# An encoder layer on one core: tiles at multiples of 512 bytes, late v and bias tables, and the second FFN matrix mixed in four products

## The chip, the cores and the metric

The kernel runs on one core of a Trainium2 chip. The metric is the device time of one execution in microseconds (us). Work is done by five engines with queues of their own: TensorE (PE, matmuls; the loading of its stationary operand is shown apart as PEld), VectorE (DVE), ScalarE (ACT), GpSimd (POOL) and SyncE (SP), whose queue here issues nearly all DMA transfers. Engines wait for each other by semaphores.

## The reference

One layer of an encoder, 1024 tokens of width 1024, float32:

```python
mod = c_act @ w_ada[l] + b_ada[l]                      # shifts, scales and gates: sh1 sc1 gt1 sh2 sc2 gt2
h = rms_norm(x, g_norm1[l]) * (1.0 + sc1) + sh1
proj = h @ w_in[l]                                     # q, k, v of both attentions, and the gates
o_a = neighbourhood_attention(qa, ka, va, rpb[l])      # 8 heads, with a table of biases
outs, lses = dilated_window_attention(...)             # 3 groups of 4 heads
o_b = einsum('gbsh,gbshd->bshd', softmax(lses), outs)  # "combine"
gate_a, gate_b = split(sigmoid(gates + b_gate[l]))
merged = gate_a * (o_a @ w_proj_a[l]) + gate_b * (o_b @ w_proj_b[l])
x = x + gt1 * (merged @ w_o[l])
h2 = rms_norm(x, g_norm2[l]) * (1.0 + sc2) + sh2
a, up = split(h2 @ w_ffn_in[l])                        # d_ff = 2816
x = x + gt2 * ((silu(a) * up) @ w_ffn_out[l])
```

## The kernel before

Matrices are multiplied as sums of three products of split halves: `wsplit` makes of a float32 tile a rounded tile `whi` (on ACT, L108) and the rest `wlo` (on POOL or DVE, L109), and `PASS` runs hi x hi, hi x lo and lo x hi into one bank of PSUM. A matmul has a stationary operand of 128 columns and a moving operand of up to 512.

The stages, in order of time:

- Attention, to about 616 us. Ten units u (two heads each; kinds 0 to 2 are the dilated groups, kind 3 the neighbourhood attention) of eight token tiles t; n = 8u + t counts the steps. Each step projects one tile of q, k and v (L293) and, between its matmuls, runs the scores (L451, L518), transposes (L477, L543) and value products (L492, L563) of an earlier unit. DVE also works off the adaLN matrix (`ada_step`: loads `wa` by L276, accumulates by L282). The results of kinds 0 to 2 are combined by `combine_prep` and `combine_step` (transposes L647) from step n = 63 on.
- Gates (L687, L706), projections of the attention outputs (L1095, moving tile oT), output projection (L1237, moving tiles wr and whi, wlo), to 876 us.
- First FFN product (L1301, moving tiles h2T and t), to 1302 us. Both FFN products use a fast scheme with seven block products in place of eight; t are mixed blocks of h2T.
- Second FFN product (L1471), to the end: seven products, numbered n = 0 to 6 in `PRODS`, each of 11 steps k, each step 12 matmuls. Products 0 to 2 use blocks of the second matrix as they are; products 3 to 6 use mixes of them, made by `w2_mix(k)`: four loads `m` on SP (L1445) and four subtractions on DVE (L1447 to L1450), called inside products 1 and 2. `finish` multiplies a finished block by the gate (DVE, L1492), adds x (POOL, L1493) and stores it.

PE's order is the order of the code. For ACT, DVE, POOL and SP a scheduler sets the order, except where instructions are pinned by `pin`, which keeps them in program order.

Memory: a pool on the left begins where the pool left of it ends, a pool on the right ends where the pool right of it begins. Counted from a multiple of 512 bytes, the tiles of the left pools (raw, whi, wlo, hT, h2T) begin at byte 320. Those of the right pools begin at 480 in the stages behind attention (tg, oT, wr, sg, the mixed t, e, m), and in attention at 352 (qk, PT, and all tiles of tag "big") or 416 (P, stg), with qn at 0. All right-hand tiles of 512-column matmuls lie above byte 139,000 of a partition, all left-hand ones under 122,000.

The tag "big" has eight slots of 4 KB, which v, the bias tables `rb`, `wa2`, `tp`, `gsig` and others take in turn. A new unit takes its slot for v, and for kind 3 two slots for the bias tables, when it begins (t = 0); v is written to memory tile by tile and read back into that slot at t = 7 (L340, L344).

## Time and profile before

| | |
|---|---|
| median of 3 runs | 1522.92 us (1522.58 to 1523.85) |
| profiled execution | 1524.07 us, its span 1522.3 us |
| PE busy | 1499.0 us, 98% of the span |
| DVE / ACT / POOL busy | 1101.9 / 657.4 / 538.4 us |
| granted TensorE clock, mean | 0.998 |
| memory traffic | 241.66 MB, 159 GB/s over the span |

The span runs from the first to the last instruction; the execution's time has about 2 us more around it. A duration of a matmul in the trace is longer than the time until the next one starts, because matmuls are pipelined: the time that a stage takes follows from start to start, or from a window's length over the count of matmuls in it.

### The profile page before, as it was taken

The page shows a single profiled execution, that of the slowest core. Times are in us where ns is not written, and L with a number is a line of the kernel's source. Part 1 is how long each engine was busy: PE and PEld are TensorE (multiplying, and loading weights), DVE is VectorE, ACT ScalarE, POOL GpSimd, SP SyncE. Part 2 cuts the span into 40 slices and gives each one's busy share as a digit, 9 for nine tenths or more (in the row PEclk, how much of TensorE's full clock was granted, in tenths as well). Part 3 has the DMA queues.
Part 4 walks back from the last instruction along what each step waited for, and adds up shares of the span by engine and source line. Part 5 has one row for each costly group of instructions (what it writes and reads, how often), then busy time and mean ns, then how long its engine had stood idle before and what let it go on. Part 6 is the DMA issues. An engine that isn't in the chain of part 4 may idle for free. (4 is left out here: it accounts for less than half of the span.)

```text
span 1522.3 us, 24290 instructions
## 1 busy us (share of the span) xinstructions
PE 1499.0 (98%) x8156; PEld 1267.7 (83%) x8156; DVE 1101.9 (72%) x2318; ACT 657.4 (43%) x1638; POOL 538.4 (35%) x540
## 2 busy tenths in 40 slices
PE   9999999999999999999999999999999999999998
PEld 7999989998888877788888888888888888887886
DVE  6868777767899845466665596788777777599468
ACT  5555555554544543236432354333222233344442
POOL 0432333311101040002342301677777775104464
PEclk9999999999999999999999999999999999999999
DMA  9625544535245165824562225345533334798342
GB/s 369 231 76 184 158 148 150 175 124 166 73 138 149 61 202 155 304 83 126 165 217 101 93 89 177 127 132 170 174 107 104 105 107 141 268 365 285 99 153 97
DMA packets 154414, 241.66 MB, mean 159 GB/s; under 512 B 26656, under 2 KB 73376, under 8 KB 153520
## 3 DMA queue, kind: packets, MB, share of 16 engines
q1 hardware_dynamic: 153136, 235.90, 47.5%
q10 hardware_dynamic: 1152, 4.19, 0.7%
q8 instruction: 65, 1.06, 0.3%
q14 instruction: 61, 0.50, 0.1%
HBM read 179.89 MB, written 60.15 MB: 158 GB/s over the span
## 5 line engine op out<-in xcount | busy, mean ns | idle before, releaser
L109 POOL TENSOR_TENSOR wlo<-raw,whi 128x512 fp32r<-128x512 f32 (+2 forms) x133 | 173.0, 1314 | 469.4 <-ACT whi L108 417.6
L108 ACT ACTIVATE whi<-raw 128x512 fp32r<-128x512 f32 (+1 forms) x348 | 204.3, 600 | 282.7 <-PE ps_s L1471 33.6
L293 PE MATMUL ps_d<-whi,hT 128*128 128x384 f32 x1152 | 311.7, 342 | 0.3 <-ACT vs L331 0.3
L109 DVE TENSOR_TENSOR wlo<-raw,whi 128x512 fp32r<-128x512 f32 (+1 forms) x215 | 181.8, 857 | 77.2 <-ACT whi L108 72.0
L293 PEld LDWEIGHTS ps_d<-whi,hT 128*128 128x128 f32 x1152 | 210.4, 189 | 5.8 <-ACT vs L331 4.1
L293 PE MATMUL ps_d<-wlo,hT 128*128 128x384 f32 x576 | 193.9, 337 | 2.2 <-DVE wlo L109 1.9
L293 PEld LDWEIGHTS ps_d<-wlo,hT 128*128 128x128 f32 x576 | 109.0, 189 | 3.0 <-DVE wlo L109 2.2
L108 ACT ACTIVATE whi<-ws 128x512 fp32r<-128x512 f32 x65 | 40.9, 629 | 130.3 <-DVE ws L1318 76.6
L1251 POOL TENSOR_TENSOR e<-e,c 128x512 f32<-128x512 f32 x44 | 68.6, 1560 | 64.3 <-DVE c L1381 40.1
L109 POOL TENSOR_TENSOR wlo<-m,whi 128x512 fp32r<-128x512 f32 x35 | 51.6, 1484 | 54.0 <-ACT whi L108 54.0
L323 POOL TENSOR_TENSOR ra<-qn,rtab 128x64 f32<-128x64 f32 x48 | 16.2, 338 | 150.8 <-DVE qn L316 132.1
L530 ACT ACTIVATE P<-P,st 128x256 f32<-128x256 f32 (+2 forms) x100 | 45.5, 456 | 40.6 <-DVE st L528 40.6
L687 PE MATMUL ps_d<-hT,whi 128*128 128x512 f32 x192 | 60.5, 396 | 0.0
L1301 PE MATMUL ps_v<-h2T,whi 128*128 128x512 f32 x192 | 59.3, 390 | 0.0
L1301 PE MATMUL ps_s<-h2T,whi 128*128 128x512 f32 x192 | 59.2, 390 | 0.0
L466 ACT ACTIVATE P<-P,sx 128x384 f32<-128x384 f32 (+1 forms) x64 | 37.0, 578 | 51.4 <-DVE sx L465 51.4
L1249 ACT ACTIVATE e<-e 128x512 f32<-128x512 f32 x44 | 27.4, 630 | 71.9 <-DVE e L1384 47.4
L282 DVE SCALAR_TENSOR_TENSOR acc<-wa,cact,acc 128x512 f32<-128x512 f32 x56 | 42.0, 749 | 20.6 <-DMA wa<-in_wada_dram 20.4
L1301 PE MATMUL ps_d<-h2T,whi 128*128 128x512 f32 x184 | 56.8, 390 | 0.0
L109 DVE TENSOR_TENSOR wlo<-ws,whi 128x512 fp32r<-128x512 f32 x45 | 50.5, 1123 | 8.2 <-ACT whi L108 8.2
L119 ACT ACTIVATE ry<-ss,eps 128x4 f32<-128x4 f32 (+1 forms) x88 | 26.3, 299 | 67.4 <-DVE ss L314 65.2
L1250 DVE TENSOR_TENSOR e<-e 128x512 f32<-128x512 f32 x44 | 42.6, 975 | 17.3 <-ACT e L1249 17.1
(445 smaller groups left out, 3968.9 us busy)
## 6 DMA issues: line engine op xcount, KB each, us to landing
raw<-in_w_dram SPq DMA_DIRECT2D x139, 256.0 KB
ga_d<-e SPq DMA_DIRECT2D x77, 256.0 KB
raw<-ga_d SPq DMA_DIRECT2D x77, 256.0 KB
wa<-in_wada_dram SPq DMA_DIRECT2D x32, 512.0 KB
raw<-in_wqkv_dram SPq DMA_DIRECT2D x80, 192.0 KB
m<-in_w_dram SPq DMA_DIRECT2D x44, 256.0 KB
raw<-in_wg_dram SPq DMA_DIRECT2D x42, 256.0 KB
xt<-in_x_dram SPq DMA_DIRECT2D x16, 512.0 KB
```

Of the source, the lines that this page charges most:

```text
L108: nc.scalar.activation(hi[:, :n], r, AF.Copy)
L109: (eng or nc.gpsimd).tensor_sub(lo[:, :n], r, fview(hi[:, :n]))
L119: nc.scalar.activation(y, ss, AF.Ln, scale=1.0 / n, bias=eps)
L282: nc.vector.scalar_tensor_tensor(ada_acc[c], wa, cact[:, kk:kk + 1], ada_acc[c], op0=ALU.mult, op1=ALU.add)
L293: nc.tensor.matmul(pd[:, :384], tok(a, k, t), U.w[k][b][:, :384], start=(k == 0 and i == 0), stop=(k == KT - 1 and i == 2))
L466: nc.scalar.activation(P[:nq, :nk], P[:nq, :nk], AF.Exp, scale=-1.0, bias=nm, accum_out=sm)
L530: nc.scalar.activation(C.P[h][:nq, c], C.P[h][:nq, c], AF.Exp, scale=-1.0, bias=nm, accum_out=sm)
L687: nc.tensor.matmul(st["p"], gw[i, br][j][a][:, kk * 128:(kk + 1) * 128], hT[b][:, k, hs], start=(k == 0 and q == 0), stop=(k == 7 and q == 2))
L1249: nc.scalar.activation(sg, a, AF.Sigmoid)
L1250: nc.vector.tensor_mul(sg, sg, a)
L1251: nc.gpsimd.tensor_mul(sg, sg, up)
L1301: nc.tensor.matmul(pb, w[p][:, k * 128:(k + 1) * 128], b[q][:, k], start=(k == 0 and i == 0), stop=(k == 3 and i == 2))
```

## The change

It has three parts.

1. Alignment. A pool `edge` of 480 bytes is put at the right end, `rg` moves to the front of the constants, and fillers of 192, 384 and 32 bytes (`fill`) stand in the pools const, attn and wo; in attn the tags of P, PT, qn and others are taken in a fixed order at the start (`place`). With that all tiles of 512 bytes and more begin at a multiple of 512 bytes.
2. Late tables. For kinds 1 to 3 the slot of v is taken at t = 7, when v is read back, and the bias tables are taken and loaded at t = 5 (`RBT`) by `bias_tabs`. The combine begins at n = 64 (`COMB`) instead of 63.
3. Second FFN matrix. The eleven mixes are called at the steps of `MIXAT`, which lie in products 0 to 3 instead of 1 and 2. The first finished block, `finish(0, 0, c11)`, moves from behind the second product to behind the adds of the fourth, with its multiplications pinned.

```diff
+EDGE, CFILL, AFILL, OFILL = 480, 192, 384, 32
-PAIRED = 58
+PAIRED, RBT, COMB = 58, 5, 64
...
+    edge = pool("edge", "right")
+    edge.tile([128, EDGE // 4], F32, name="edge")
...
+    def fill(p, n, name):
+        p.tile([128, n // 4], F32, name=name)
...
+    rg = const.tile([128, 2, 2, 16], F32, name="rg")
+    fill(const, CFILL, "cfill")
...
+    for tag, n, bufs in (("bm", 512, 1), ("p", 512, 4), ("qn", 256, 7), ("rtab", 512, 1), ("acc2", 512, 1), ("pT", 512, 4),
+                         ("stg", 512, 3), ("vs", 128, 2), ("ra", 64, 2), ("rb", 64, 2)):
+        ap_.tile([128, n], F32, tag=tag, bufs=bufs, name="place")
...
+            if t == 7:
+                U.v = big("v", [128, 8, 128])
...
-        U.v = big("v", [128, 8, 128])
+        if U.kind == 0:
+            U.v = big("v", [128, 8, 128])
...
             U.bias = []
-            for h in range(2):
-                b = big("rb", [128, 768])
-                nc.sync.dma_start(b, rbias[U.pair * 2 + h])
-                U.bias.append(b)
         return U
+
+    def bias_tabs(U):
+        for h in range(2):
+            b = big("rb", [128, 768])
+            nc.sync.dma_start(b, rbias[U.pair * 2 + h])
+            U.bias.append(b)
...
-        ci = n - (8 * 7 + 7)
+        ci = n - COMB
...
             proj_post(U, t)
+            if U.kind == 3 and t == RBT:
+                bias_tabs(U)
+
+    fill(ap_, AFILL, "afill")
...
+    fill(wop, OFILL, "ofill")
...
+    MIXAT = tuple((n, k) for n, ks in enumerate(((4, 6, 8, 10), (2, 5, 8), (1, 4, 7), (1,))) for k in ks)
...
-            if n in (1, 2) and k % 2 == n - 1:
-                w2_mix((k + (n - 1) * HT) // 2)
+            if (n, k) in MIXAT:
+                w2_mix(MIXAT.index((n, k)))
...
-    def finish(rh, c, z, last=None):
+    def finish(rh, c, z, last=None, late=False):
...
-            nc.vector.tensor_mul(z[m], z[m], gt2[:, cs])
+            mul = nc.vector.tensor_mul(z[m], z[m], gt2[:, cs])
+            if late:
+                pin(mul)
...
     p2 = prod2(1)
     for m in range(4):
         add(c11[m], c21[m], p2[m])
-    finish(0, 0, c11)
...
     for m in range(4):
         add(c21[m], c21[m], p6[m])
         add(c12[m], c12[m], p6[m])
+    finish(0, 0, c11, late=True)
```

The order of SP at the first bias tables (end of the dilated units, about 314 us in the trace of before): v read back, the bias loads `rb`, the adaLN loads `wa`, and the stores of v's tiles `v_d`. Before:

```order
L340 DMA v<-v_d 128x1024
L398 DMA rb<-in_rbias_dram 128x768 x2
L276 DMA wa_4789<-in_wada_dram 128x1024
L276 DMA wa_4947<-in_wada_dram 128x1024
L333 DMA v_d<-vs 128x128
L276 DMA wa_5117<-in_wada_dram 128x1024
```

After (lines of the changed file: L354 is L340, L288 is L276, L416 is L398, L345 is L333):

```order
L354 DMA v<-v_d 128x1024
L288 DMA wa_4799<-in_wada_dram 128x1024
L288 DMA wa_4957<-in_wada_dram 128x1024
L288 DMA wa_5127<-in_wada_dram 128x1024
L416 DMA rb<-in_rbias_dram 128x768
L345 DMA v_d<-vs 128x128
L416 DMA rb<-in_rbias_dram 128x768
```

Three `wa` loads now stand ahead of the bias loads; the next unit (about 365 us) has the same exchange.

The order of SP at the mixes in the second FFN product: `raw<-ga_d` and `raw<-in_w` are the two operands of one step, `m` the loads of a mix. Before, from the operands of a step of product 1:

```order
L101 DMA raw<-ga_d 128x512
L101 DMA raw<-in_w_dram 128x512
L1445 DMA m_0_14800<-in_w_dram 128x512
L1445 DMA m_0_14801<-in_w_dram 128x512
L1445 DMA m_0_14802<-in_w_dram 128x512
L1445 DMA m_0_14803<-in_w_dram 128x512
L101 DMA raw<-ga_d 128x512
L101 DMA raw<-in_w_dram 128x512
```

After, at the operands of the same kind (L1467 is L1445); ahead of these rows stand the eight loads of m_0 and m_1:

```order
L1467 DMA m_2_14761<-in_w_dram 128x512
L1467 DMA m_2_14762<-in_w_dram 128x512
L1467 DMA m_2_14763<-in_w_dram 128x512
L1467 DMA m_2_14764<-in_w_dram 128x512
L1467 DMA m_3_14821<-in_w_dram 128x512
L1467 DMA m_3_14822<-in_w_dram 128x512
L1467 DMA m_3_14823<-in_w_dram 128x512
L1467 DMA m_3_14824<-in_w_dram 128x512
L111 DMA raw<-ga_d 128x512
L111 DMA raw<-in_w_dram 128x512
```

The loads of four mixes, sixteen, now stand in a row between the operands of two steps, where four stood.

POOL at the finish of c11: the adds `c<-c,x` and the splits `wlo<-m`. Before:

```order
L1260 TENSOR_TENSOR e<-e 128x512
L1493 TENSOR_TENSOR c_14496<-c_14496,x_15128 128x512
L1493 TENSOR_TENSOR c_14497<-c_14497,x_15133 128x512
L1493 TENSOR_TENSOR c_14498<-c_14498,x_15138 128x512
L1493 TENSOR_TENSOR c_14499<-c_14499,x_15143 128x512
L109 TENSOR_TENSOR wlo<-m_0_14802,whi 128x512
```

After (L1518 is L1493, L119 is L109):

```order
L119 TENSOR_TENSOR wlo<-m_5_14997,whi 128x512
L1518 TENSOR_TENSOR c_14513<-c_14513,x_15731 128x512
L1518 TENSOR_TENSOR c_14514<-c_14514,x_15736 128x512
L1518 TENSOR_TENSOR c_14515<-c_14515,x_15741 128x512
L1518 TENSOR_TENSOR c_14516<-c_14516,x_15746 128x512
L119 TENSOR_TENSOR wlo<-m_6_15081,whi 128x512
```

The four adds come 16 splits later, in the middle of those for the fifth product.

## The prediction

> **What bounds the kernel now.** I read the busy shares on the page first, then the windows by stage, then the waits of TensorE (PE), and last the durations of its matmuls by tile. The page and the windows (core, stretch, length and busy time of each engine, with the number of instructions):

> ```profile
> span 1522.3 us, 24290 instructions
> PE 1499.0 (98%) x8156; PEld 1267.7 (83%) x8156; DVE 1101.9 (72%) x2318; ACT 657.4 (43%) x1638; POOL 538.4 (35%) x540
> ...
> 314.00:530.00 216.00, 207.51 (x1463) 183.66 (x1462) 175.83 (x599) 109.99 (x381) 16.42 (x15) 0.99 0.39 119
> 616.00:1302.00 686.00, 685.10 (x3003) 558.96 (x3003) 484.51 (x640) 242.92 (x423) 320.48 (x222) 1.00 0.43 140
> 1302.00:1522.00 220.00, 212.00 (x929) 173.51 (x927) 162.11 (x213) 88.05 (x150) 83.61 (x56) 0.99 0.63 215
> ```

> PE is busy for 98% of the span and, in the gates, projections and first FFN product (616 to 1302), for 685.10 of 686 us (the row from 616). There is nothing to win there by a shorter wait; only shorter matmuls help. Outside, PE idles 8.49 us of attention's second half and 8.00 us of the last FFN stage. The waits of PE that the change could reach (us in total, times, longest):

> ```profile
> PE ps_t L477 <- DVE P L469: 2.6, 2, 1.8
> PE ps_d L1471 <- DVE wlo L109: 2.6, 3, 2.1
> PE ps_t L647 <- DVE PT L481: 1.8, 3, 1.3
> PE ps_t L647 <- ACT PT L483: 1.7, 1, 1.7
> PE ps_t L477 <- DVE rv L120: 1.3, 2, 0.8
> ```

> **Part 1, the alignment.** It adds no instruction; it moves start addresses. What that can change is in the durations of matmuls by tile (line, tiles, count: minimum/median/maximum ns). All of these move 512 columns; the moving tile is h2T, t, oT, wr, tg, or the whi and wlo of L1471.

> ```profile
> L1301 PE MATMUL ps_v<-h2T,whi x192: 389/389/476, 875.9 to 1302.5; 128*128 128x512 f32 x192
> L1471 PE MATMUL ps_d<-whi x88: 388/389/397, 1302.9 to 1511.7; 128*128 128x512 f32 x88
> L1301 PE MATMUL ps_v<-t,whi x136: 392/394/401, 945.8 to 1291.4; 128*128 128x512 f32 x136
> L1301 PE MATMUL ps_s<-t,wlo x64: 392/397/400, 951.8 to 1275.1; 128*128 128x512 f32 x64
> L1095 PE MATMUL ps_t<-oT,whi x64: 392/397/400, 714.3 to 775.7; 128*128 128x512 f32 x64
> L1095 PE MATMUL ps_s<-oT,wlo x16: 392/397/400, 721.8 to 781.5; 128*128 128x512 f32 x16
> L1237 PE MATMUL ps_d<-wr,h2T x90: 392/397/477, 781.8 to 863.7; 128*128 128x512 f32 x90
> L1237 PE MATMUL ps_v<-wr,h2T x60: 392/397/477, 808.1 to 851.7; 128*128 128x512 f32 x60
> L706 PE MATMUL ps_d<-tg,whi x40: 392/394/400, 642.3 to 700.1; 128*128 128x512 f32 x40
> L706 PE MATMUL ps_v<-tg,wlo x12: 392/398/400, 662.1 to 697.5; 128*128 128x512 f32 x12
> ```

> The median is 389 ns where the moving tile is in a left pool; where it is in a right pool, not even the minimum is under 392. Left pools begin at byte 320 of a 512-byte block, right ones of these stages at 480: the first is a multiple of 64, the second is 32 past one. Matmuls overlap, so their price is start to start. Two windows filled by one kind each give it, oT first and then whi and wlo of L1471:

> ```profile
> 719.00:775.00 56.00, 56.00 (x241) 45.02 (x240) 40.30 (x57) 25.82 (x42) 25.40 (x20) 1.00 0.49 159
> 1400.00:1500.00 100.00, 100.00 (x443) 82.84 (x442) 64.30 (x77) 42.26 (x74) 58.43 (x41) 1.00 0.42 130
> ```

> A window counts what touches it, and a 389 ns matmul at this spacing adds about 1.7: 56.00/239.3 is 234.0 ns, 100.00/441.3 is 226.6. The difference, 7.4 ns, fits the durations (medians of 394 to 398 against 389). By groups (first and last are quoted) the slow kind counts 792 with t (8 groups), 288 with oT (8), 240 with wr (3) and 180 with tg (8): 1500 matmuls. At 7.0 ns, a little under the difference since some of the fast ones too stray upward, that is 10.5 us. All of it lies in the windows in which PE never waits, so all of it is on the path; DVE and POOL keep room there (third and fifth pair of the row).

> What speaks against it: the same tiles are those at high addresses, so that the region and not the 32 bytes may be the cause, and then moving them by 32 bytes gives nothing. And the score matmuls move keys from byte 352, also 32 past a multiple of 64 and high, at the median of the projection's matmuls of the same 384 columns, which move whi from a left pool:

> ```profile
> L451 PE MATMUL ps_s<-qk x192: 274/335/445, 365.0 to 598.9; 64*128 64x384 f32 x144, 64*128 64x256 f32 x48
> L293 PE MATMUL ps_d<-whi,hT x1152: 334/334/522, 67.9 to 524.9; 128*128 128x384 f32 x192
> ```

> These run two at a time on half the rows each, so their pace may have another limit; and being high as well, they speak as much against the region as against the 32 bytes. The bounds are 0 and 11.1 us (1500 at 7.4); I take 10.5, since the step from 389 to 392 has no exception. The left pools move from 320 to 0, both multiples of 64: I book nothing for them. [...]

> **Part 2, late v and bias tables.** The 8 slots of tag "big" are shared by v, bias, adaLN weights (wa) and others. Before, a unit takes v's slot at its first tile and its bias loads (2 of 384 KB) stand on SP ahead of the wa loads. The vector engine (DVE) then stands at L282, and P's normalization L469, for which PE waits, is queued behind it:

> ```profile
> 371.93 0.75 DVE L282 SCALAR_TENSOR_TENSOR acc<-wa,cact,acc 128x512 f32<-128x512 f32 x1 [4.39 <-DMA wa<-in_wada_dram]
> 372.60 0.35 DVE L469 TENSOR_SCALAR P<-P,sx 128x256 f32<-128x256 f32 x1
> ```

> ```profile
> DVE acc L282 <- DMA wa<-in_wada_dram: 20.4, 12, 5.8
> ```

> After, wa goes first on SP. Two bias tables are 0.77 MB; at the 367 GB/s of a saturated stretch (quoted below) they took 2.1 us. Moving them behind shortens the 4.39 us wait by about that, and the 2.6 us of L477 behind L469 falls to about 0.6: 2.0 us gained. The longest wait of L282, 5.8 us, stands one unit earlier behind the same two loads, but PE loses little there; I add 0.3 us for it. Against that stands the combine, which moves one slot later: its transposes L647 wait 1.8 + 1.7 us now and may wait more or less, plus or minus 1.7. The bias tables, now issued at the sixth tile, are used by scores of the next unit, several tiles later: cover of over 10 us, nothing booked. The v loads stay at the eighth tile; their slot was taken long before and may now be held when they come: nothing booked, up to a rival. I take -2.3; the bounds are -5.6 (the waits of L477 and L647 quoted, 7.4 us, without half of L647's) and +3.5 (L647's waits double and nothing is gained).

> **Part 3, FFN2.** 44 m loads of 256 KB, 44 mix subtractions and 4 muls and 4 adds of the finish are moved, none added. Before, mixes (products 2 and 3) and the finish of block c11 meet; the timeline of DVE (start, length, instruction), of POOL and of PE (in brackets what it idled before):

> ```profile
> 1369.69 1.78 DVE L1447 TENSOR_TENSOR m<-m,m 128x512 f32<-128x512 f32 x1
> 1371.40 1.28 DVE L1492 TENSOR_TENSOR c<-c,gt 128x512 f32<-128x512 f32 x2
> 1372.60 3.45 DVE L109 TENSOR_TENSOR wlo<-raw,whi 128x512 fp32r<-128x512 f32 x2
> ```

> ```profile
> 1369.24 1.68 POOL L1493 TENSOR_TENSOR c<-c,x 128x512 f32<-128x512 f32 x1 [1.83 <-DVE c L1492]
> 1372.15 3.34 POOL L1493 TENSOR_TENSOR c<-c,x 128x512 f32<-128x512 f32 x2 [1.23 <-DMA m<-in_w_dram]
> ```

> ```profile
> 1376.10 0.50 PE L1471 MATMUL ps_d<-wlo,whi 128*128 128x512 f32 x1 [2.06 <-DVE wlo L109]
> 1382.12 0.50 PE L1471 MATMUL ps_d<-wlo,whi 128*128 128x512 f32 x1 [0.28 <-DVE wlo L109]
> ```

> The window that ends there:

> ```profile
> 1340.00:1372.00 32.00, 32.00 (x143) 26.51 (x142) 30.62 (x47) 15.10 (x24) 2.97 (x2) 1.00 1.04 379
> ```

> DVE is full (30.62 of 32 us), and beside POOL's adds its 0.68 us operations take up to 1.8 (L1447, and two of L109 take 3.45): 4 x 0.68 of muls and about 3.2 us of stretching go away from there. PE then loses neither 2.06 nor 0.28 us: 2.3. The finish lands behind product 4, in the window from 1400 quoted above, where DVE is busy for 64 and POOL for 58 of 100 us; its adds, 1.3 to 1.7 us each, fit behind wlo of L109 made several steps ahead.

> What is late next is the loads. SP's new order has 16 m loads in a row ahead of the raws of product 2's third step, where 4 stood. They begin at 1320.2:

> ```profile
> L1445 SPq DMA_DIRECT2D m<-in_w_dram x44: 327/416/1797, 1320.2 to 1385.1; - x44
> DMA packets 9257, 16.90 MB, mean 367 GB/s; under 512 B 1029, under 2 KB 1029, under 8 KB 9253
> ```

> A load takes 0.262 MB/367 = 0.71 us when DMA is full (the second row is that of 1326 to 1372). 18 of them and about 2 us of latency end at 1335.0; splitting takes 0.62 on ACT and 0.68 on DVE, and about 0.4 of queue: 1336.7. PE gets there after 13 steps of 2.72 us (12 x 226.6 ns); the first starts at 1302.9 (the row of L1471), so that makes 1338.3. The next step has four m loads ahead of its raws too: 1336.7 + 6 x 0.71 = 1341.0, against 1341.0. So the cover is about gone: a stall of 0 to 3 us, and I take 0.8, as the loads that other queues put between are not counted. Part 3: -2.3 + 0.8 = -1.5, bounds -2.3 and +0.7.

> **The sum.** -10.5 - 2.3 - 1.5 = -14.3 us. The profiled execution took 1524.07, 1.15 over the median of the runs; from the median, 1522.92 - 14.3 = 1508.6, so 1508.6 us. This case's own range is 1504 (all low ends, -19.0) to 1513 (part 1 as taken, the other two together at +0.6, half of the way to their upper ends). What tells a measurement of this kernel from no change is about 0.2%, 3.0 us.

> **Rivals.**
> Region, not alignment: the 1500 matmuls keep 234.0 ns. For it speaks that no tile in this trace is aligned and high, and the qk row; against it, that the whole step sits in the minimum of tiles in four different stages. Time: 1522.92 - 3.8 = 1519.1 (1515 to 1523). [...]

> Alignment beyond 64 bytes: matmuls from left tiles, now at byte 320, get faster as well at byte 0. If they gained as much as the right ones, 7 ns, the 924 of L1471 (77 steps of 12) alone would add 6.5 us: 1502 or below. Against it: in the rows above nothing from a left tile falls under 388 ns, and their medians are their minima, so that none of them looks delayed.

> Slower, by the v slots: eight v transfers stand on SP at the eighth tile of each unit of kinds 1 to 3 and now wait for a slot that others hold; the raws of the next unit stand behind them, and PE at the next unit's first tile. This turns the sign when it costs the 8 units 14.3 + 3.0 us, 2.2 us each, more than any single wait of PE quoted above; at 2.5 us each the time is 1522.9 - 14.3 + 20 = 1528.6. Against it: earlier wa loads free their slots sooner, and the number of slots is the same.

> **Chances.** Forecast 0.75, region 0.17, beyond 64 bytes 0.04, slower 0.03, anything else 0.01. The region's case ends more than 3.0 us faster about six times in ten, so faster is 0.75 + 0.04 + 0.10 = 0.89, same 0.07 + 0.01, slower 0.03. The range takes the forecast's own 1504 and the middle of the region's case, 1519.5: outside are 0.04, 0.03, some 0.07 of the region's and 0.04 of the forecast's tails.

> **What will show it.** Part 1: minimum 389 for t, oT, wr and tg, and about 239 to 247 matmuls in 56 us of oT. If 392 stays, the region was it. Part 2: L477's wait on L469 under 1 us, L282's waits on wa well under 20.4 us in all; a new wait of PE on v or hT's raws would be the rival. Part 3: no wait of L1471 in product 3 (1372 to 1386), and one near product 2's third to fifth step (1336 to 1346 less what part 1 and 2 gain ahead of it) of at most 3 us. The prediction is wrong if the sum of PE's idle time grows, or if the right tiles keep their duration.

## The result, and the profile after

The changed kernel takes 1513.48 us (median of 5 runs, 1512.08 to 1517.73) against 1522.92 us before (5 runs, 1522.58 to 1524.86): a ratio of 0.9938, 95% interval 0.9922 to 0.9954, 9.4 us less. The forecast was 14.3 us less. The profiled execution took 1513.48 us; its span is 10.6 us shorter than that of before, and the share and sum of PE's busy time say that all of it is busy time:

```profile
span 1511.7 us, 24292 instructions
...
PE 1488.2 (98%) x8156; PEld 1268.4 (84%) x8156; DVE 1102.9 (73%) x2318; ACT 657.5 (43%) x1638; POOL 538.7 (36%) x540
```

PE is busy for 10.8 us less, and it idles for 23.5 us, as before (23.3). By stages, from the first matmul of each (gates from 525.1 us before and 527.7 after, L706 from 616.5 and 619.1, second FFN product from 1302.9 and 1293.5, last matmul's start at 1516.2 and 1506.8):

| stage | before | after | difference | forecast |
|---|---|---|---|---|
| attention | 525.1 | 527.7 | +2.6 | -2.3 |
| gates L687 | 91.4 | 91.4 | 0 | 0 |
| L706 to L1301 | 686.4 | 674.3 | -12.1 | -10.5 |
| second FFN product, and end of the span | 219.4 | 218.2 | -1.2 | -1.5 |

Part 1, durations by tile (line numbers are those of the changed file: L1323 is L1301, L1116 is L1095), and the window that is filled with oT:

```profile
L1323 PE MATMUL ps_v<-h2T,whi x192: 389/389/476, 872.8 to 1293.0; 128*128 128x512 f32 x192
L1323 PE MATMUL ps_v<-t,whi x136: 389/389/389, 942.6 to 1282.1; 128*128 128x512 f32 x136
L1116 PE MATMUL ps_t<-oT,whi x64: 389/389/389, 715.1 to 774.5; 128*128 128x512 f32 x64
```

```profile
619.00:1293.00 674.00, 673.54 (x3004) 558.08 (x3003) 485.00 (x640) 241.45 (x423) 321.36 (x222) 1.00 0.43 142
720.00:775.00 55.00, 55.00 (x245) 45.53 (x244) 41.22 (x57) 25.01 (x41) 23.08 (x19) 1.00 0.48 158
```

The 392 to 400 ns are gone: minimum, median and maximum are 389, and 55.00/243.3 is 226.1 ns from start to start where 234.0 stood. Parts 2 and 3 show in PE's waits (L494 is L477, L1494 is L1471, L119 is L109; L672 and L675 are the combine's accumulation on DVE):

```profile
PE ps_t L494 <- DVE oacc L672: 2.8, 1, 2.8
PE ps_v L1494 <- DVE wlo L119: 2.2, 2, 1.3
PE ps_t L494 <- DVE P L486: 2.1, 2, 1.2
...
PE ps_t L494 <- DVE oacc L675: 1.9, 1, 1.9
```

The waits of the combine's transposes (1.8 and 1.7 us before) are nearly gone, and new ones stand in their place. Behind three of these waits, PE's clock is halved, in the clock record to 0.5 for 3.41 us each (stretch, length, PE busy, granted clock, DMA share, GB/s):

```profile
372.00:376.00 4.00, 2.66 (x10) 0.74 0.53 207
376.00:380.00 4.00, 4.00 (x21) 0.84 0.06 16
428.00:432.00 4.00, 3.73 (x15) 0.57 0.48 163
488.00:492.00 4.00, 3.49 (x16) 0.74 0.35 116
492.00:496.00 4.00, 4.00 (x26) 0.83 0.78 239
```

Where it is 0.5, the 384-column matmuls of L305 start every 320 ns, against 173 at full clock. What each of the three costs is estimated by (1 - clock) x length: 1.7 us. Before, there was one such place in this stage, at 372 to 380. In both profiles PE idles for 10.6 us between 100 us and the gates, so the new waits only take the place of old ones. By that estimate the 2.6 us that attention lost are 3.4 us more at half clock, less 0.8 us elsewhere. Slow matmuls count as busy time, so the idle time alone doesn't show this loss.

### The profile page after: what moved, and what is told of

Same layout as the page of the kernel before. It is cut to its first block, busy times and chain, and to the rows that moved or that the text cites. A ratio compares the mean times of both kernels' runs of the same rounds, so it can differ in the third digit from the quotient of the medians.

```text
span 1511.7 us, 24292 instructions
## 1 busy us (share of the span) xinstructions
PE 1488.2 (98%) x8156; PEld 1268.4 (84%) x8156; DVE 1102.9 (73%) x2318; ACT 657.5 (43%) x1638; POOL 538.7 (36%) x540
## 4 chain that ended last, share of the span: by engine, by line
PE 85%; DMA 6%; DVE 5%; issue 1%; ACT 1%; SPq 1%; POOL 1%; DVEq 0%; POOLq 0%; ACTq 0%
PE ps_d L305 16%; PE ps_v L1323 7%; PE ps_d L1323 7%; PE ps_s L1323 7%; PE ps_t L1323 6%; PE ps_d L704 4%; PE ps_v L1494 3%; PE ps_t L1494 3%; PE ps_s L1494 3%; PE ps_d L1494 3%; PE ps_s L1258 2%; PE ps_d L1258 2%; DMA wa<-in_wada_dram 2%; PE ps_v L1258 1%; PE ps_v L1116 1%
## 5 line engine op out<-in xcount | busy, mean ns | idle before, releaser
L119 POOL TENSOR_TENSOR wlo<-raw,whi 128x512 fp32r<-128x512 f32 (+2 forms) x133 | 172.9, 1314 | 466.6 <-ACT whi L118 437.1
L305 PE MATMUL ps_d<-whi,hT 128*128 128x384 f32 x1152 | 312.7, 343 | 0.0
L119 DVE TENSOR_TENSOR wlo<-raw,whi 128x512 fp32r<-128x512 f32 (+1 forms) x215 | 180.7, 856 | 68.8 <-ACT whi L118 67.3
L305 PEld LDWEIGHTS ps_d<-whi,hT 128*128 128x128 f32 x1152 | 211.6, 190 | 5.2 <-ACT vs L343 3.5
L305 PE MATMUL ps_d<-wlo,hT 128*128 128x384 f32 x576 | 194.5, 338 | 2.4 <-DVE wlo L119 2.0
L305 PEld LDWEIGHTS ps_d<-wlo,hT 128*128 128x128 f32 x576 | 109.5, 190 | 3.2 <-DVE wlo L119 2.3
L119 POOL TENSOR_TENSOR wlo<-m,whi 128x512 fp32r<-128x512 f32 x35 | 51.4, 1479 | 105.2 <-ACT whi L118 103.8
L335 POOL TENSOR_TENSOR ra<-qn,rtab 128x64 f32<-128x64 f32 x48 | 16.7, 349 | 153.0 <-DVE qn L328 138.0
L1271 ACT ACTIVATE e<-e 128x512 f32<-128x512 f32 x44 | 27.5, 630 | 91.4 <-DVE e L1406 64.0
L294 DVE SCALAR_TENSOR_TENSOR acc<-wa,cact,acc 128x512 f32<-128x512 f32 x56 | 43.4, 775 | 26.8 <-DMA wa<-in_wada_dram 26.8
L483 ACT ACTIVATE P<-P,sx 128x384 f32<-128x384 f32 (+1 forms) x64 | 37.1, 580 | 51.9 <-DVE sx L482 51.9
L1323 PE MATMUL ps_v<-h2T,whi 128*128 128x512 f32 x192 | 59.2, 389 | 0.0
L1323 PE MATMUL ps_s<-h2T,whi 128*128 128x512 f32 x192 | 59.1, 389 | 0.0
L1323 PE MATMUL ps_d<-h2T,whi 128*128 128x512 f32 x184 | 56.7, 390 | 0.0
L119 DVE TENSOR_TENSOR wlo<-ws,whi 128x512 fp32r<-128x512 f32 x45 | 50.2, 1116 | 8.0 <-ACT whi L118 8.0
L1272 DVE TENSOR_TENSOR e<-e 128x512 f32<-128x512 f32 x44 | 42.5, 974 | 16.7 <-ACT e L1271 16.5
```

The lines of the kernel that those rows point to most:

```text
L119: (eng or nc.gpsimd).tensor_sub(lo[:, :n], r, fview(hi[:, :n]))
L294: nc.vector.scalar_tensor_tensor(ada_acc[c], wa, cact[:, kk:kk + 1], ada_acc[c], op0=ALU.mult, op1=ALU.add)
L305: nc.tensor.matmul(pd[:, :384], tok(a, k, t), U.w[k][b][:, :384], start=(k == 0 and i == 0), stop=(k == KT - 1 and i == 2))
L483: nc.scalar.activation(P[:nq, :nk], P[:nq, :nk], AF.Exp, scale=-1.0, bias=nm, accum_out=sm)
L1272: nc.vector.tensor_mul(sg, sg, a)
L1323: nc.tensor.matmul(pb, w[p][:, k * 128:(k + 1) * 128], b[q][:, k], start=(k == 0 and i == 0), stop=(k == 3 and i == 2))
```

## The experiments

Twelve kernels ran in three rounds, each round on one chip beside the kernel before; ratios are to that kernel, so kernels of different rounds are compared by their ratios or by their traces. The first six concern the addresses.

**Alignment alone.** All edits of part 1 and none of the others; the instructions stand in the order of before on every engine.

> The kernel before with part 1 alone: all tiles at multiples of 512 bytes, the order of every queue that of before. If the start address is what makes t, oT, wr and tg slow, their matmuls have 389 ns again and the stages from 616 to 1302 us lose about 12 us in all (the changed kernel lost 1.8 + 2.2 + 1.8 + 6.3 there): 1522.9 - 12 = about 1511 us, with the waits of the attention and of the second FFN product as before. Rival: part of that came from the other two parts, and the time is 1513 us or more.

1509.72 us (1507.06 to 1510.54), ratio 0.9903 (0.9887 to 0.9919): faster than the whole change. L706 to L1301 take 673.7 us, 12.7 less than before, with t and oT at 389 ns throughout. Part 1 accounts for the whole gain and more.

**Parts 2 and 3 on the old addresses.**

> Parts 2 and 3 alone on the old addresses, the order of every queue that of the changed kernel. If the changed kernel lost the missing 5 us in the attention by itself (its start of the gates was 2.6 us later than before, with two more stretches at a granted clock of about 0.5), this one is as slow there: 1522.9 + 2.6 - 1.2 at the end = about 1524 us, between 1522 and 1526. Rival: the faster matmuls caused the new waits, and parts 2 and 3 on the old addresses gain what was forecast for them, 3.8 us: 1519 us.

1525.91 us (12 runs, 1521.53 to 1529.70), ratio 1.0014 (1.0002 to 1.0026): a little slower, as the first reading said. Attention ends at 528.4 us in its profile, with waits on `oacc` at the same two places as in the changed kernel (1.4 us at 428, 2.9 at 490). The faster matmuls did not cause them.

**An edge of 32 bytes.** Is 64 bytes the grain, as the prediction had it?

```diff
+    edge = pool("edge", "right")
+    edge.tile([128, 8], F32, name="edge")
```

> The kernel before with one edge of 32 bytes at the right end and nothing else: right tiles go from byte 480 to 448 of a 512-byte block, a multiple of 64 and not of 128 or more; left tiles stay at 320; the order is that of before. If 64 bytes are the grain, t, oT, wr and tg have 389 ns and the time is that of full alignment, about 1511 us. If 128 or 512 bytes are needed, they keep 392 to 400 ns and the time stays at about 1522 us.

1521.46 us, ratio 0.9987 (0.9974 to 1.0001). The moving tiles begin at byte 448, a multiple of 64, and are about as slow as at 480 (L1303 is L1301, L1097 is L1095):

```profile
L1303 PE MATMUL ps_v<-t,whi x136: 387/394/398, 945.8 to 1290.7; 128*128 128x512 f32 x136
L1097 PE MATMUL ps_t<-oT,whi x64: 387/394/398, 714.9 to 776.1; 128*128 128x512 f32 x64
```

So a start at a multiple of 64 bytes isn't enough: the cause that the prediction named is wrong.

**Left tiles moved away.** The changed kernel, with whi, wlo, hT and h2T at byte 480 and the right tiles left at 0.

```diff
-EDGE, CFILL, AFILL, OFILL = 480, 192, 384, 32
+EDGE, CFILL, AFILL, OFILL = 480, 160, 384, 32
```

> The changed kernel with the filler of the constants at 160 instead of 192 bytes: left tiles (whi, wlo, hT, h2T) at byte 480 instead of 0, right ones stay at 0; the order is that of the changed kernel. If a start 32 past a multiple of 64 costs 7.4 ns wherever the tile lies, the 512-column matmuls that move whi, wlo, hT or h2T (about 2650) get medians of 394 to 398 ns: +19.6 us, and if the 1776 of 384 columns in the projection pay as much, +13 us more: 1533 to 1546 us. If high addresses are needed for the loss, they keep 389 ns and the time stays at about 1513 us.

1524.95 us (one run), and neither expectation: the moved tiles stay fast and those that were not moved become slow.

```profile
L1323 PE MATMUL ps_v<-h2T,whi x192: 387/389/476, 877.6 to 1304.9; 128*128 128x512 f32 x192
L1323 PE MATMUL ps_v<-t,whi x136: 393/395/399, 947.6 to 1293.8; 128*128 128x512 f32 x136
L1116 PE MATMUL ps_t<-oT,whi x64: 393/395/399, 716.2 to 777.4; 128*128 128x512 f32 x64
```

h2T with whi, both at 480, is fast; t at 0 with whi at 480 is slow. What all runs up to here have in common is the distance from the start of the stationary tile to that of the moving one: 0 is fast (both at 0, 320 or 480, medians of 389 ns), while 32, 128 and 160 are slow (medians of 394 to 398). In these runs neither the byte itself nor the region of the memory tells the fast tiles from the slow ones.

**Edges of 160 and 416 bytes** test that distance. With 160, t, oT, wr and tg stand at 320 like whi; with 416, they stand at 64, 256 away.

> The kernel before with one edge of 160 bytes at the right end and nothing else; the order is that of before. Right tiles behind attention (tg, oT, wr, t) then begin at byte 320 of a 512-byte block, as the left ones do; neither is a multiple of 128. Theory of the run with moved left tiles: a matmul is slow when its moving tile and the stationary tile that is loaded beside it begin at different bytes of a 512-byte block. Then all of them have 389 ns and the time is that of full alignment, 1509.7 us, within 2 us. Rival: both must begin at a multiple of a larger power of two; then t, oT, wr and tg keep about 233 ns from start to start and the time is about 1521 us.

> The same with an edge of 416 bytes: right tiles at byte 64, 256 away from the left ones at 320. If what counts is the distance within 256 bytes, t, oT, wr and tg start every 226 to 227 ns and the time is 1507 to 1512 us; if it is the distance within 512 bytes, they keep 230 to 238 ns and it is 1517 to 1524 us.

```profile
L1303 PE MATMUL ps_v<-t,whi x136: 389/389/389, 941.2 to 1280.8; 128*128 128x512 f32 x136
L1097 PE MATMUL ps_t<-oT,whi x64: 389/389/389, 712.4 to 771.8; 128*128 128x512 f32 x64
```

```profile
L1303 PE MATMUL ps_v<-t,whi x136: 389/389/389, 938.4 to 1278.0; 128*128 128x512 f32 x136
L1097 PE MATMUL ps_t<-oT,whi x64: 389/389/389, 710.9 to 770.3; 128*128 128x512 f32 x64
```

The first fence is 160, the second 416; both are fast throughout. 160 took 1513.40 us (6 runs, ratio 0.9940, 0.9925 to 0.9955), 416 took 1509.54 (one run). So one tile of 416 bytes, with everything else as before, gives in its one run what the whole alignment gives, and in these runs a distance of 256 bytes is as good as 0 (389 ns), while 128 is not (394). That 160 is 3.7 us behind alignment alone (the intervals of the ratios don't overlap) is not explained by these matmuls: in its profile L706 to L1301 take 676.1 us, 1.9 of them waits. One of 0.9 us before L706 is in the kernel before too, one of 0.9 us before L1237 in no other profile. The rest of the difference stays open.

**The combine at n = 63 again**, everything else as changed.

```diff
-PAIRED, RBT, COMB = 58, 5, 64
+PAIRED, RBT, COMB = 58, 5, 63
```

> The changed kernel with the combine at n = 63 again; alignment, late tables and the new FFN order stay. If the later combine puts its DVE work (oacc) ahead of the normalization that the transposes of L494 wait for, the waits of 2.8 and 1.9 us on oacc are gone, and the stretches of halved clock behind them: about 4.7 + 3.4 us less, some 3 us of the old waits of the combine's transposes come back: 1509 to 1511 us. Rival: the late tables cause these waits; then 1513 us as the changed kernel.

1511.55 us, ratio 0.9927 (0.9915 to 0.9939) against the changed kernel's 0.9938. The waits on oacc are gone and attention ends at 525.3 us instead of 527.7; the intervals of the two ratios overlap, so the 2 us rest on the traces. There, the four profiles with the combine at n = 64 have attention end between 527.5 and 528.4 us, the two with late tables and n = 63 at 525.3 and 525.7. The mechanism is in DVE's timeline of the changed kernel (L294 is L282):

```profile
424.84 1.54 DVE L294 SCALAR_TENSOR_TENSOR acc<-wa,cact,acc 128x512 f32<-128x512 f32 x2 [4.51 <-DMA wa<-in_wada_dram]
426.29 0.68 DVE L672 TENSOR_TENSOR oacc<-ut,ps_t 128x512 f32<-128x512 f32 x1
```

DVE stands at L294 until its `wa` has landed; behind it is queued the `oacc` that empties the bank which the transposes L494 need, and PE waits 2.85 us for it. At n = 63 that pair does not meet.

**Late tables alone** (aligned, combine at 63, FFN order of before).

> Alignment and the late v and bias tables, with the combine at n = 63 and the FFN order of before. If the late tables give nothing because the adaLN step L294 is only queued earlier on DVE and waits for wa as long as before (4.5 to 5.6 us against 4.3), the time is that of alignment alone, 1509.7 us, within 1.5 us, and PE's waits between 365 and 376 us add up to 2.5 us or more. If they gain the 2.3 us that were forecast, it is 1507.4 us.

1510.43 us, ratio 0.9927 (0.9915 to 0.9940), not faster than alignment alone, and its attention ends at 525.7 us against 523.1. Counted from the start of v's loads ahead of it, `wa` is issued 1.0 us earlier than before and has landed 2.4 us earlier, about as forecast, but DVE takes the step earlier as well. The place that the prediction quoted, in the changed kernel:

```profile
368.28 0.75 DVE L294 SCALAR_TENSOR_TENSOR acc<-wa,cact,acc 128x512 f32<-128x512 f32 x1 [4.52 <-DMA wa<-in_wada_dram]
```

4.52 us of waiting where 4.39 stood. L282 now stands ahead of the scores' minimum (L482) instead of behind it, so that with late tables alone PE's wait is spread over two links (0.6 us at L468, 1.8 at L494) and not removed. The 2.6 us that this attention is longer than that of alignment alone don't show a cost of the late tables: PE idles for 8.8 us between 100 us and the gates against 9.2, and the difference is 5.1 us against 1.7 lost at half clock. The edge of 32 bytes, with the tables of before, lost 5.1 us as well.

**Part 3 undone, and part 3 alone.**

> The changed kernel with the mixes at their old steps and the finish of c11 behind the second product again. If the sixteen loads in a row cost the 2.2 to 2.5 us of waits that the changed kernel has in its second product (its 1329 to 1335 us), these go, and the old wait in the third product comes back with 0.4 us (as in the kernel with alignment alone) to 2.3 us (as before): 1511 to 1513.5 us. If part 3 gains what was forecast, 1.5 us, the time is 1515 us.

1512.63 us, ratio 0.9940 (0.9926 to 0.9953): the same as the changed kernel. The 1.3 us wait in the third product came back for the two in the second.

> Alignment and part 3 (mixes in four products, late finish), with early tables and the combine at n = 63. If the sixteen loads in a row cost 2.0 to 3.2 us in the second product and the old wait in the third, 0.4 to 1.3 us on aligned tiles, is all that is saved, the time is 1510 to 1513 us. If part 3 gains the 1.5 us that were forecast, it is about 1508 us.

1511.57 us, ratio 0.9930 (0.9918 to 0.9942): 1.9 us more than alignment alone by the medians, with intervals that overlap a little. PE's waits in its second product (1.4 and 0.95 us) are those of the changed kernel. In the changed kernel's timelines of PE, of SP and of DVE (L1467 is L1445, L1469 to L1472 are L1447 to L1450):

```profile
1331.00 0.50 PE L1494 MATMUL ps_v<-wlo,whi 128*128 128x512 f32 x1 [1.28 <-DVE wlo L119]
1334.99 0.50 PE L1494 MATMUL ps_v<-wlo,whi 128*128 128x512 f32 x1 [0.97 <-DVE wlo L119]
```

```profile
1311.22 10.92 SPq L1467 DMA_DIRECT2D m<-in_w_dram  x16
1322.47 0.33 SPq L111 DMA_DIRECT2D raw<-ga_d  x1
```

```profile
1328.45 0.69 DVE L1471 TENSOR_TENSOR m<-m,m 128x512 f32<-128x512 f32 x1
1329.06 0.68 DVE L119 TENSOR_TENSOR wlo<-raw,whi 128x512 fp32r<-128x512 f32 x1
1329.66 0.68 DVE L1472 TENSOR_TENSOR m<-m,m 128x512 f32<-128x512 f32 x1
1330.27 0.68 DVE L119 TENSOR_TENSOR wlo<-raw,whi 128x512 fp32r<-128x512 f32 x1
```

The sixteen loads hold SP for 10.9 us; only then are the operands of the third step issued. ACT begins to split them at 1327.91, after 3.73 us of waiting for `raw<-ga_d`. DVE is then among the subtractions of four mixes: each of the two splits has one ahead of it, and the second is done at 1330.95, when PE goes on.

**Only the finish moved** (aligned, attention and mixes in the order of before).

> Alignment with the mixes at their old steps and only the finish of c11 behind the fourth product. No sixteen loads in a row, so no wait in the second product; without POOL's adds beside the mixes the wait of L1494's counterpart in the third product, 0.4 to 1.3 us, goes as well: 1508.5 to 1509.5 us, 0.2 to 1.2 under alignment alone. If the mixes and not the finish make that wait, it stays and so does the time, 1509.7 us.

1506.60 us (4 runs, 1503.59 to 1508.92), ratio 0.9896 (0.9881 to 0.9912): the fastest of all, 6.9 us under the changed kernel. Its second FFN product has no wait beyond 0.26 us:

```profile
1288.00:1499.00 211.00, 210.74 (x928) 173.51 (x926) 163.46 (x211) 88.39 (x150) 84.22 (x56) 1.00 0.65 222
```

So the finish, with POOL's adds beside the mixes, made the wait of the third product, and moving it removes that wait. Against alignment alone the ratios' intervals overlap; what the traces show of this stage, from its first matmul's start to its last one's, is 210.0 us against 211.7. Other profiles agree: from the third product's first matmul to the fourth's it is 31.7 to 33.2 us in the seven kernels with the early finish (33.2 in the kernel before), and 29.9 to 30.0 in the six with the late one and at most one mix behind the third product.

**Mixes spread** over the second to fourth product (aligned, late finish, attention in the order of before).

```diff
-    MIXAT = tuple((n, k) for n, ks in enumerate(((4, 6, 8, 10), (2, 5, 8), (1, 4, 7), (1,))) for k in ks)
+    MIXAT = tuple((n, k) for n, ks in enumerate(((), (1, 4, 7, 10), (1, 4, 7, 10), (1, 3, 5))) for k in ks)
```

> Alignment, the finish of c11 behind the fourth product, and the mixes at steps 1, 4, 7, 10 of the second and third product and 1, 3, 5 of the fourth: never more than four loads in a row between the operands of two steps, and eight mixes instead of eleven where DVE is full. Neither the wait of the second nor that of the third product should be there: 1508.5 to 1509.5 us, the shortest of all. If the loads of four are already too many beside the operands, a wait of up to 1 us shows in the second product.

1517.19 us (7 runs), ratio 0.9965 (0.9951 to 0.9978), a miss: the second product is free of waits, but the third and fourth are not.

```profile
PE ps_d L1490 <- DVE wlo L119: 3.5, 4, 1.6
PE ps_v L1490 <- DVE wlo L119: 2.9, 3, 2.0
```

```profile
1384.77 1.77 DVE L1465 TENSOR_TENSOR m<-m,m 128x512 f32<-128x512 f32 x1
1386.57 1.69 DVE L1466 TENSOR_TENSOR m<-m,m 128x512 f32<-128x512 f32 x1
1388.29 1.64 DVE L1467 TENSOR_TENSOR m<-m,m 128x512 f32<-128x512 f32 x1
```

The last mixes now run in the fourth product, where POOL splits m tiles, and DVE's subtractions take 1.6 to 1.8 us there instead of 0.68. The splits of the next operands are queued behind them. In the third product, where POOL is idle, DVE stands for 3.9 us (to 1359.45) and 3.2 us (to 1379.32) at a subtraction whose loads haven't landed, again with a split behind it. By this trace a mix should run where POOL is idle and its loads have landed; that was not run.

## Why the prediction was right or wrong

The sign was right, and the measured 1513.48 us lies in the stated range (1504 to 1519.5), but this owes something to luck: it lies above the forecast's own upper end, 1513, and below the rival's range from 1515, and is covered because the range was drawn out for that rival. (The 1513 has a slip: half of the way from -3.8, which is -2.3 - 1.5, to the upper ends, +4.2 together, is +0.2 and not +0.6, so that the end is 1512.6.) The sum was 4.9 us off. By the stages of the profiles, attention missed by 4.9 us, L706 to L1301 gave 1.6 more than booked, and the last stage came within 0.3; the other 1.15 are the profile of before, which was that much above its median.

- Part 1, the count and the price: right, and a little low. 1500 matmuls at 7.0 ns were booked as 10.5 us; the stages lost 12.1 us in the changed kernel and 12.7 with alignment alone, of which 0.4 and 0.9 are waits of PE. All of it was on the path, as argued. The price was put under the 7.4 ns of the windows because some of the fast matmuls stray upward, but these strays went away as well: with h2T, 108 of 1054 started 231 ns or more apart before, and 6 after.
- Part 1, the cause: wrong. "32 past a multiple of 64" fell with the edge of 32 bytes; the rival, the region, fell with the moved left tiles. The step that failed was to compare the moving tiles only: in the trace of before, a moving tile at 480 always has its stationary tile at 320, so that its byte, its region and its distance can't be told apart there. The score matmuls, which the prediction kept as evidence against, move and load from one tile, distance 0, and at a median of 335 ns against 334 they are not slow, which agrees with the distance; that was not run by itself.
- Part 2, -2.3 us: wrong in sign, +2.6 us in the profiles. That moving the bias loads "shortens the 4.39 us wait by about that" took DVE's order as given; the step moved up the queue with its data, and DVE's waits on wa add up to 26.8 us where 20.4 stood. The combine's later slot, booked as "plus or minus 1.7", opened waits of 2.8 and 1.9 us. PE's idle time as a whole stayed, and what makes the +2.6 is the half clock behind the waits.
- The clock was in no term. By the estimate above, a wait near 2 us can cost 1.7 us more: in the changed kernel single idle gaps of 2.85 and 1.85 us have a drop of the clock behind them. In the clock records of before and after it falls to exactly 0.5, away from the end of the span for 3.41 us each time; in rows of 4 us of all fourteen profiles, (1 - clock) x length at one place adds up to 1.7 us or to twice that.
- Like waits cost differently. In the changed kernel the three drops begin at 373.89, 428.51 and 489.95 us, 54.61 and 61.44 us apart, which are 16 and 18 times 3.413. When these two traces are cut into stretches of 3.413 us, with an end wherever a drop begins, PE idles in the stretches ahead of the drops for 1.71 us before and for 2.27, 1.93 and 1.86 us in the changed kernel; the idlest ones from 100 to 1490 us with no drop behind them have 1.67 us before and 1.72 in the changed kernel. The latter holds 1.72 us of a gap of 2.02 us at 211.77; the rest lies in the next stretch. That the idle time within one stretch decides, and so where a gap falls, is the author's estimate from these figures; no run tested it. In the row from 372 to 376 us PE idles for 2.91 us in the kernel with the finish alone and the clock stays at 1.00 there and in the next row; with the edge of 160 bytes it idles for 2.85 us and the next row has 0.57. In the times the clock shows as well: the five runs of the changed kernel lie between 1512.08 us at a mean clock of 0.998 and 1517.73 at 0.993; but the five with late tables alone all have 0.996 and lie between 1509.79 and 1515.37, so that the clock is not all of the spread.
- Part 3: -1.5 us were booked, and the FFN product itself gained nothing (213.3 and 213.4 us from its first matmul's start to its last one's). That the stage came within 0.3 us is luck: the end of the span behind the last matmul's start shrank from 6.1 to 4.9 us, which no term covered. The finish was right: the third product went from 33.2 to 29.9 us, 3.3 less where 2.3 were booked. But the second went from 30.0 to 33.3. "A stall of 0 to 3 us, and I take 0.8" was the mis-sized term: 2.2 to 2.5 us of waits and 3.3 us in the product. The third step's operands were there 16.7 us after the first of the sixteen loads began, not 14.8, since the DMA moved 6.4 MB in that time, as much as 24 such loads, and the sum counted 18. The latency, booked at about 2 us, is near what the trace of before shows for its first load, the small cp (issued at 0.74 us, ACT goes on with it at 2.44). DVE's queue, booked at 0.4 us, cost more, too: the splits were ready 3.0 us after that and not 1.7.

## What to carry to other kernels

Compare the durations of one and the same matmul by tile. Here they differed by 5 to 9 ns (389 against 394 to 398) in a stage in which PE hardly waits, the placement of the tiles cost 12.1 us over 1500 matmuls, and one filler of 416 bytes took that back (1509.54 us, one run). Test each part of a bundle alone: here one part of three gave the whole gain, half of another was worth 2 to 3 us, and the sixteen loads and the later combine gave that back. A wait shortened on paper stayed (4.52 us where 4.39 stood), as the instruction that waits moved up its queue together with its data.
